# PEER block: 32 of 256 tokens taken out of the dense expert products, and V's rows as the stationary side

## The chip, the core and the metric

The kernel runs on one core of a Trainium2 chip. The core has five engines that run side by side: TensorE (PE; matrix products, with its weight loads shown apart as PEld), VectorE (DVE), ScalarE (ACT), GpSimd (POOL) and SyncE (SP), which here only issues transfers. All DMA queues share 16 DMA engines. The metric is device time in microseconds (us) of one execution; less is better.

## The reference

One decoder block for 256 tokens of width 1024: two token mixers with gates and a residual, then an expert layer (PEER) and a final norm. The change concerns the expert layer:

```python
qh = (x_blk @ w_q).reshape(tc, PEER_HEADS, 2, PEER_HALF)
scores = jnp.einsum('thpc,hpnc->thpn', qh, skf)          # 8 heads x 2 x 128 keys
s_top, i_top = lax.top_k(scores, PEER_TOPK)              # 16 of 128, twice per head
cand = s_top[:, :, 0, :, None] + s_top[:, :, 1, None, :]
c_s, c_pos = lax.top_k(cand.reshape(...), PEER_TOPK)     # 16 of 256 pairs
e_idx = ...                                              # 16 of 16384 experts per head
g = jax.nn.softmax(c_s, axis=-1)
u, v = expert_u[e_idx], expert_v[e_idx]
a = jax.nn.gelu(jnp.einsum('td,thkd->thk', x_blk, u), approximate=False)
return jnp.einsum('thk,thkd->td', g * a, v)
```

So each token uses 128 of 16384 experts, each a row of U and a row of V of 1024 numbers. Everything is float32; the answer must hold to float32 products.

## The kernel before

The kernel doesn't fetch the chosen rows. It computes all 16384 experts for all 256 tokens, in 128 blocks of 128 experts, and multiplies by a weight that is zero where an expert was not chosen.

**Precision.** TensorE's fast format, f32r, keeps part of a float32. `split` (lines 92 to 100) makes a first part `hi` on ScalarE (line 96) and the rest `lo` = source - hi on VectorE or GpSimd (line 99). A product is the sum hi*hi + hi*lo + lo*hi.

**U pass** (lines 607 to 648). Per block b: `load` fetches 512 KB of U (SyncE's queue, four `raw` buffers) and splits it; `mm3` (line 112) does 24 products, 8 chunks of the width by 3, with U as the stationary side (128 columns of weights each) and the tokens `xh`, `xl` as the moving side (256 columns); ScalarE applies GELU into `W[:, b]` (128 experts by 256 tokens, kept in SBUF for all blocks). Between blocks VectorE works on the top-16 search (`topk_steps`): first tokens 128 to 255, then 0 to 127. An allowance per block, `EARLY_RATE` before the scatter and `TOPK_RATE` after it, sets how many steps of the search are written behind each block. VectorE's order is the written order here (`manual_schedule`); the other engines' queues are ordered by the scheduler. Until the scatter is written, the rest of every second block goes to GpSimd (line 613).

**Weights of experts.** For tokens 128 to 255 GpSimd scatters the 128 x 128 weights into a table `gd` in memory that is zero elsewhere (line 469: 128 indirect transfers, each head behind the one before). For tokens 0 to 127 `g_build` makes them on TensorE, four tokens a group: 32 groups, line 581, four products each, spread over the later blocks; `g_use` multiplies them into `W`.

**V pass** (lines 695 to 712). Per block: `weigh` fetches the table's part (line 663) and multiplies it into `W` for tokens 128 to 255 (line 667); `W[:, b]` is split into `xhi`, `xlo`; V's block is loaded and split into `whi`, `wlo`; 12 products (line 675) with `W` as the stationary side (128 tokens) and V as the moving side (512 columns) add up in four accumulators, tokens by width. The last three blocks' products are sorted by accumulator, and `finish` (residual, sum of squares, norm, output) of the first 128 tokens runs under the products of the second.

## Time and profile before

| | us |
|---|---|
| median of 3 runs (1012.6 to 1015.11) | 1013.67 |
| the profiled execution | 1012.72 |
| its span, first to last instruction | 1010.9 |
| TensorE busy in it | 986.2 |
| VectorE, ScalarE, GpSimd busy | 732.4, 580.8, 305.1 |

A timeline row has start, duration, engine, line, operation, tiles (out<-in), shape and how many were merged; in brackets, the idle time before it and who ended it. A source row has count, ns min/median/max and first and last start. A row by stretches has its bounds and length, then busy us (and instructions) of each engine in the order PE, PEld, DVE, ACT, POOL, or of those engines alone that have the line that was asked for (line 99: DVE, POOL), then TensorE's granted clock (1.00 is 2.4 GHz), the DMA engines' busy share and GB/s. A plain f32 product is recorded as two passes, an f32r product as one.

### The profile page before, as it was taken

How to read it: one execution, taken by the hardware profiler on the slowest of the kernel's cores; microseconds unless marked ns; L12 is line 12 of the kernel's file. 1: busy time of each engine (PE TensorE's matmuls, PEld its weight loads, DVE VectorE, ACT ScalarE, POOL GpSimd, SP SyncE). 2: the span in 40 equal slices, each digit the busy share in tenths (PEclk: the TensorE clock that was granted, in tenths of full speed). 3: DMA queues.
4: the chain of work that ended last, by engine and by line, in shares of the span. 5: the costliest groups of instructions: out<-in, count | busy, mean ns of one | idle time of the engine just before them, and what ended most of it. 6: DMA issues, size and time to landing. Idle time of an engine off the chain costs nothing.

```text
span 1010.9 us, 17560 instructions
## 1 busy us (share of the span) xinstructions
PE 986.2 (98%) x6571; PEld 891.0 (88%) x6571; DVE 732.4 (72%) x1417; ACT 580.8 (57%) x1042; POOL 305.1 (30%) x210
## 2 busy tenths in 40 slices
PE   8999999999998999999999999999999999999996
PEld 7898899799998999999999999888888888888884
DVE  6566767764888988779789898766666666666665
ACT  5564546543564555778778777544444444444444
POOL 0000000000344878877877876001011010101010
PEclk9999999999999999999999999999999999999998
DMA  7667685545554877767667666766666666666662
GB/s 242 216 210 246 193 262 180 179 146 168 160 180 148 208 188 188 169 167 169 166 150 186 155 180 162 235 213 215 208 214 210 214 208 215 208 221 210 213 211 73
DMA packets 73557, 194.23 MB, mean 192 GB/s; under 512 B 25472, under 2 KB 25984, under 8 KB 73344
## 3 DMA queue, kind: packets, MB, share of 16 engines
q1 hardware_dynamic: 50400, 181.95, 57.3%
q0 software_dynamic: 21504, 8.47, 7.1%
q10 hardware_dynamic: 1568, 2.70, 0.8%
q8 instruction: 51, 0.84, 0.3%
q14 instruction: 34, 0.28, 0.1%
HBM read 183.58 MB, written 9.50 MB: 191 GB/s over the span
## 4 chain that ended last, share of the span: by engine, by line
PE 89%; DVE 5%; issue 2%; ACT 2%; DMA 1%; POOL 1%; ACTq 0%; DVEq 0%; POOLq 0%
PE pj L112 44%; PE acc L675 35%; PE pj L231 5%; DVE wlo L99 1%; PE gp L581 1%; ACT whi L96 1%; PE sps L412 1%; ACT JR L573 1%; POOL wlo L99 1%; DVE W L456 0%; DMA W<-in_consts_dram 0%; PE s L302 0%; DMA ident<-in_consts_dram 0%; PE tp L165 0%; PE z L250 0%
## 5 line engine op out<-in xcount | busy, mean ns | idle before, releaser
L96 ACT CAST whi<-raw 128x1024 fp32r<-128x1024 f32 x327 | 343.5, 1051 | 353.2 <-issue 195.9
L99 DVE TENSOR_TENSOR wlo<-raw,whi 128x1024 fp32r<-128x1024 f32 x315 | 386.4, 1228 | 168.4 <-ACT whi L96 164.0
L112 PE MATMUL pj<-xh,whi 128*128 128x256 f32 x1280 | 310.4, 282 | 2.9 <-ACT whi L96 2.9
L112 PE MATMUL pj<-xl,whi 128*128 128x256 f32 x1280 | 308.7, 280 | 0.1
L469 POOL DMA_INDIRECT gd<-gS,iS x128 | 239.0, 1867 | 66.9 <-issue 36.3
L112 PEld LDWEIGHTS pj<-xh,whi 128*128 128x128 f32 x1280 | 241.3, 189 | 5.0 <-ACT whi L96 4.1
L112 PEld LDWEIGHTS pj<-xl,whi 128*128 128x128 f32 x1280 | 241.5, 189 | 0.7 <-DVE xl L172 0.4
L112 PE MATMUL pj<-xh,wlo 128*128 128x256 f32 x1280 | 180.5, 282 | 6.0 <-DVE wlo L99 3.8
L112 PEld LDWEIGHTS pj<-xh,wlo 128*128 128x128 f32 x1280 | 162.1, 188 | 10.1 <-DVE wlo L99 6.8
L675 PE MATMUL acc<-whi,xlo 128*128 128x512 f32 x512 | 161.7, 395 | 0.7 <-DVE xlo L99 0.7
L675 PE MATMUL acc<-wlo,xhi 128*128 128x512 f32 x512 | 161.4, 394 | 0.0
L675 PE MATMUL acc<-whi,xhi 128*128 128x512 f32 x512 | 139.9, 395 | 0.5 <-ACT xhi L96 0.5
L663 POOL DMA_DIRECT2D gq<-gd x64 | 34.5, 540 | 326.3 <-DVE W L667 306.2
L675 PEld LDWEIGHTS acc<-whi,xlo 128*128 128x128 f32 x512 | 96.3, 188 | 24.1 <-DVE xlo L99 1.6
L99 POOL TENSOR_TENSOR wlo<-raw,whi 128x1024 fp32r<-128x1024 f32 x12 | 30.9, 2574 | 285.5 <-ACT whi L96 271.7
L675 PEld LDWEIGHTS acc<-whi,xhi 128*128 128x128 f32 x512 | 96.3, 188 | 23.5 <-ACT xhi L96 1.1
L675 PEld LDWEIGHTS acc<-wlo,xhi 128*128 128x128 f32 x512 | 96.5, 188 | 22.5
L620 ACT ACTIVATE W<-pj 128x256 f32<-128x256 f32 (+24 forms) x128 | 44.3, 347 | 19.2 <-PE pj L112 19.1
L99 DVE TENSOR_TENSOR xlo<-W,xhi 128x256 fp32r<-128x256 f32 x128 | 53.6, 419 | 0.7 <-ACT xhi L96 0.7
L96 ACT CAST xhi<-W 128x256 fp32r<-128x256 f32 x128 | 51.5, 403 | 2.3 <-DVE W L667 2.3
L573 ACT ACTIVATE JR<-iota,njT 128x128 fp32r<-128x128 f32 x128 | 41.1, 396 | 0.0
L577 DVE TENSOR_TENSOR B<-I,g 128x1024 fp32r<-128x1024 f32 x32 | 39.3, 1227 | 1.1
(185 smaller groups left out, 917.4 us busy)
## 6 DMA issues: line engine op xcount, KB each, us to landing
raw<-in_ut_dram SPq DMA_DIRECT2D x128, 512.0 KB
raw<-in_v_dram SPq DMA_DIRECT2D x128, 512.0 KB
raw<-in_wf_dram SPq DMA_DIRECT2D x72, 512.0 KB
gd<-zfill SPq DMA_DIRECT2D x16, 512.0 KB
gq<-gd POOLq DMA_DIRECT2D x64, 128.0 KB
gd<-gS,iS POOLq DMA_INDIRECT x128
h<-in_x_dram SPq DMA_DIRECT2D x4, 256.0 KB
sks<-in_skt_dram ACTq DMA_DIRECT2D x1, 1024.0 KB
```

The costliest lines, as they stand in the source:

```text
L96: last_hi = nc.scalar.copy(hi, src)
L99: last_lo = rest.tensor_sub(lo, src, hi.bitcast(F32))
L112: nc.tensor.matmul(o, a, b, start=first and i == 0, stop=last and i == len(seq) - 1)
L231: nc.tensor.matmul(pss[tt], a[:, c, s], w[:, cc], start=k == 0 and c == 0, stop=k == 2 and c == 7)
L412: nc.tensor.matmul(sps[tt][:, mm], qt[:, tt * P:(tt + 1) * P], sks[:, m], start=True, stop=True)
L469: d = nc.gpsimd.indirect_dma_start(gd[:, :], bass.IndirectOffsetOnAxis(ap=iS[:, k:k + 1], axis=0), gS[:, k:k + 1], None, compute_op=ALU.add)
L573: nc.scalar.activation(JR[:, q], iota, AF.Abs, bias=njT[:, 4 * g + q:4 * g + q + 1])
L577: nc.vector.tensor_tensor(B, I.unsqueeze(2).to_broadcast([P, 4, 2, P]), g2[:, :, ts_].bitcast(F32).rearrange("p l t -> p t l").unsqueeze(3 ...
L581: nc.tensor.matmul(gp[:, q].rearrange("p l i -> p (l i)"), JR[:, q], B[:, q].rearrange("p l i -> p (l i)"), start=True, stop=True)
L620: gl = nc.scalar.activation(W[:, b, nd:T], ps[:, nd:T], AF.Gelu)
L663: ld = nc.gpsimd.dma_start(gq[0], gd3[:, b * P:(b + 2) * P].rearrange("j (i t) -> j i t", i=2))
L675: nc.tensor.matmul(acc[tt][hf], lhs[:, s], rhs[:, hs], start=order == 0 and b == 0, stop=order == 2 and b == NB - 1)
```

## The change

Tokens 0 to 31 leave both dense passes.

- **U pass**: the moving side is tokens 32 to 255, 224 columns; `W` has 224 columns per block, and the search's scratch in it moves. 24 groups of weights are built instead of 32. GpSimd has the rest of every block until the scatter is written, and `EARLY_RATE` is 2.4 instead of 1.45.
- **Behind the search of tokens 0 to 127**: expert numbers, gates and the normed rows of the 32 tokens are written to memory and read back spread over 128 partitions (16 tokens x 8 heads, two such groups).
- **V pass**: V's block is the stationary side, the tokens the moving side. First and rest of `W[:, b]` lie side by side in `xw`, so that `whi` meets both in one product of 448 columns, and `wlo` meets the first in one of 224; 16 products per block, into eight accumulators, width by tokens. `whi` and `wlo` have a third buffer in every third block. `xw` of block b+1 is prepared while block b runs, and the table's parts are weighed two blocks at a time.
- **The 32 tokens**: 64 gathers of 128 rows of U or V (512 KB each) on GpSimd's queue, two row buffers, one step per 1.81 blocks. VectorE multiplies and sums a row with the token (line 749), or adds a weighted row (line 761); 16 products with `sel` (128 x 16) sum the heads into the accumulators.
- **End**: each accumulator is copied (`gather_up`), turned back to tokens by width with two transposes and added to `h` (`finish`); the norm follows for all tokens at once.

```diff
@@ constants
-EARLY_RATE = 1.45
-PT = 128
+EARLY_RATE = 2.4
+S = 32
+ND = T - S
+PT = P - S
+X0 = ND - P
+GS = P // 8
@@ behind the search of tokens 0 to 127
+                    for dst, src in ((e_dr, eu), (w_dr, ge)):
+                        nc.sync.dma_start(dst.rearrange("(t e) k -> t (e k)", e=NH), src[0:S])
@@ U pass
-                    mm3(ps[:, :T], [(u_h[:, c], u_l[:, c], xh[:, c], xl[:, c]) for c in range(8)])
+                    mm3(ps[:, :ND], [(u_h[:, c], u_l[:, c], xh[:, c, S:], xl[:, c, S:]) for c in range(8)])
                     if b + 1 < NB:
-                        nxt = load(ut[b + 1], [P, 8, P], rest=nc.vector if scattered or b % 2 else nc.gpsimd)
+                        nxt = load(ut[b + 1], [P, 8, P], rest=nc.vector if scattered else nc.gpsimd)
...
+                            for e in range(NH):
+                                nc.sync.dma_start(x_dr.rearrange("(t e) (a b) -> e t a b", e=NH, a=8)[e], sxr)
+                            for dst, src in ((places, e_dr), (gates, w_dr)):
+                                nc.sync.dma_start(dst, src.rearrange("(g p) k -> p g k", g=ng))
...
-            with tc.issue_after(gl.ins):
-                nc.scalar.preload_act_table_set("natural_log_exp_and_others")
@@ V pass
+        def prepare(b):
+            w = (vp if b == NB - 1 else xsp).tile([P, 2, ND], F32R, name="xw", tag="xw")
+            nc.scalar.copy(w[:, 0], W[:, b])
+            with tc.issue_after(last_lo.ins):
+                nc.vector.tensor_sub(w[:, 1], W[:, b], w[:, 0].bitcast(F32))
+            return w
...
-            lhs, rhs = ((w_h, v_h), (w_l, v_h), (w_h, v_l))[order]
-            nc.tensor.matmul(acc[tt][hf], lhs[:, s], rhs[:, hs], start=order == 0 and b == 0,
-                             stop=order == 2 and b == NB - 1)
+            if order == 0:
+                nc.tensor.matmul(acc[c][:, S:S + 2 * ND], v_h[:, cs], w.rearrange("p a b -> p (a b)"),
+                                 start=b == 0, stop=False, skip_group_check=True)
+            else:
+                nc.tensor.matmul(acc[c][:, S:S + ND], v_l[:, cs], w[:, 0], start=False, stop=b == NB - 1,
+                                 skip_group_check=True)
...
+                    rows[n] = vp.tile([P, D], F32, name="rows", tag="rows", bufs=2)
+                    nc.gpsimd.indirect_dma_start(rows[n][:, :], None, (u_rows if kind == "u" else v_rows)[:, :],
+                                                 bass.IndirectOffsetOnAxis(ap=places[:, g, k:k + 1], axis=0))
...
+                        nc.vector.scalar_tensor_tensor(r, r, 1.0, xr, op0=ALU.mult, op1=ALU.mult,
+                                                       accum_out=a[:, g, k:k + 1])
...
+                        nc.scalar.activation(a[:, g], a[:, g], AF.Gelu)
+                        nc.vector.tensor_mul(a[:, g], a[:, g], gates[:, g])
+                        if g == ng - 1:
+                            nc.scalar.preload_act_table_set("natural_log_exp_and_others")
...
+                        nc.vector.scalar_tensor_tensor(sm, r, a[:, g, k:k + 1], sm, op0=ALU.mult, op1=ALU.add)
...
+                        nc.tensor.matmul(acc[c][:, g * GS:(g + 1) * GS], sm[:, c * P:(c + 1) * P], sel,
+                                         start=False, stop=True, skip_group_check=True)
@@ end
+            rest = vp.tile([P, T], F32, name="rest", tag="rest", bufs=3)
+            nc.gpsimd.memset(rest[:, :S], 0.0)
+            nc.scalar.copy(rest[:, S:], acc[c][:, T:T + ND])
+            nc.vector.tensor_add(rest, rest, acc[c][:, :T])
...
+                nc.tensor.transpose(tp[:, tt * P:(tt + 1) * P], rest[:, tt * P:(tt + 1) * P], ident)
+            nc.vector.tensor_add(h[:, :, cs], h[:, :, cs], tp[:, :T].rearrange("p (a b) -> p a b", a=2))
+            for tt in range(2):
+                nc.scalar.activation(sqs, h[:, tt, cs], AF.Square, accum_out=sq[:, tt, c:c + 1])
...
+        nc.scalar.activation(r, ss, AF.Ln)
+        nc.scalar.activation(r, r, AF.Exp, scale=-0.5)
```

The order of instructions moves in three places.

**Start of the U pass.** VectorE before, around the places of the scatter (`iS`); `wlo` is a rest of U's block, the steps on `W` are the search:

```order
L99 TENSOR_TENSOR wlo<-raw,whi 128x1024
L542 TENSOR_TENSOR W<-W 128x8x128
L542 TENSOR_TENSOR W<-W 128x8x64
L542 TENSOR_TENSOR W<-W 128x8x32
L543 TENSOR_TENSOR W<-W 128x128
L547 COPY gS<-W 128x128
L548 SCALAR_TENSOR_TENSOR W<-W 128x128
L549 TENSOR_SCALAR iS<-W,pcol 128x128
L99 TENSOR_TENSOR wlo<-raw,whi 128x1024
```

and VectorE now, at the same steps:

```order
L560 TENSOR_TENSOR W<-W 128x8x128
L560 TENSOR_TENSOR W<-W 128x8x64
L560 TENSOR_TENSOR W<-W 128x8x32
L561 TENSOR_TENSOR W<-W 128x128
L565 COPY gS<-W 128x128
L566 SCALAR_TENSOR_TENSOR W<-W 128x128
L567 TENSOR_SCALAR iS<-W,pcol 128x128
L472 MAX W<-sc_87 128x8 x2
L474 MAX_INDEX W<-W,sc_87 128x8 x2
L477 MATCH_REPLACE sc_87<-W,sc_87 128x128 x2
L109 TENSOR_TENSOR wlo<-raw,whi 128x1024
```

No rest of U stands among the search of the second 128 tokens any more; the first, that of block 15, stands behind half a head of the next search. GpSimd's queue before, from the rests on:

```order
L99 TENSOR_TENSOR wlo<-raw,whi 128x1024 x11
L469 DMA gd<-gS,iS 2097152x1
L99 TENSOR_TENSOR wlo<-raw,whi 128x1024
L469 DMA gd<-gS,iS 2097152x1 x127
L663 DMA gq<-gd 128x256 x64
```

and now (`rows` and `xr` are the gathers' and the token's buffers):

```order
L109 TENSOR_TENSOR wlo<-raw,whi 128x1024 x14
L487 DMA gd<-gS,iS 2097152x1 x128
L695 DMA gq<-gd 128x256 x5
L738 DMA rows<-in_ur_dram,places 128x1024 x2
L747 DMA xr<-xd 128x1024
L773 MEMSET rest 128x32 x3
L695 DMA gq<-gd 128x256 x2
L738 DMA rows<-in_ur_dram,places 128x1024 x2
```

All 14 rests stand ahead of the scatter, and the gathers share the queue with the table's parts from then on.

**A block of the V pass.** TensorE before, one block (accumulators are tokens by half the width):

```order
L675 MATMUL acc_8209<-whi,xhi 128x512
L675 MATMUL acc_8210<-whi,xhi 128x512
L675 MATMUL acc_8211<-whi,xhi 128x512
L675 MATMUL acc_8212<-whi,xhi 128x512
L675 MATMUL acc_8209<-whi,xlo 128x512
L675 MATMUL acc_8210<-whi,xlo 128x512
L675 MATMUL acc_8209<-wlo,xhi 128x512
L675 MATMUL acc_8210<-wlo,xhi 128x512
L675 MATMUL acc_8211<-whi,xlo 128x512
L675 MATMUL acc_8212<-whi,xlo 128x512
L675 MATMUL acc_8211<-wlo,xhi 128x512
L675 MATMUL acc_8212<-wlo,xhi 128x512
```

and now, the end of one block and the start of the next (accumulators are an eighth of the width by tokens):

```order
L720 MATMUL acc_8107<-xw,whi 128x448
L720 MATMUL acc_8108<-xw,whi 128x448
L723 MATMUL acc_8101<-xw,wlo 128x224
L723 MATMUL acc_8102<-xw,wlo 128x224
L723 MATMUL acc_8103<-xw,wlo 128x224
L723 MATMUL acc_8104<-xw,wlo 128x224
L723 MATMUL acc_8105<-xw,wlo 128x224
L723 MATMUL acc_8106<-xw,wlo 128x224
L723 MATMUL acc_8107<-xw,wlo 128x224
L723 MATMUL acc_8108<-xw,wlo 128x224
L720 MATMUL acc_8101<-xw,whi 128x448
L720 MATMUL acc_8102<-xw,whi 128x448
```

Products of 448 and of 224 columns come in runs of eight, each with V's columns as weights of its own. VectorE before, a block and the start of the next:

```order
L99 TENSOR_TENSOR wlo<-raw,whi 128x1024
L99 TENSOR_TENSOR xlo<-W,xhi 128x256
L667 TENSOR_TENSOR W<-W,gq 128x128
L99 TENSOR_TENSOR wlo<-raw,whi 128x1024
L99 TENSOR_TENSOR xlo<-W,xhi 128x256
```

and now, with the gathered rows' multiplies:

```order
L702 TENSOR_TENSOR W<-W,gq 128x2x128
L749 SCALAR_TENSOR_TENSOR rows,a<-rows,xr 128x1024
L709 TENSOR_TENSOR xw<-W,xw 128x224
L109 TENSOR_TENSOR wlo<-raw,whi 128x1024
L709 TENSOR_TENSOR xw<-W,xw 128x224
L109 TENSOR_TENSOR wlo<-raw,whi 128x1024
L702 TENSOR_TENSOR W<-W,gq 128x2x128
L749 SCALAR_TENSOR_TENSOR rows,a<-rows,xr 128x1024
```

The multiply of a gathered row stands ahead of the next block's `xw` and of V's next rest.

**The end.** TensorE before, from the last block's products on:

```order
L675 MATMUL acc_8210<-wlo,xhi 128x512
L675 MATMUL acc_8211<-whi,xlo 128x512
L675 MATMUL acc_8211<-wlo,xhi 128x512
L675 MATMUL acc_8212<-whi,xlo 128x512
L675 MATMUL acc_8212<-wlo,xhi 128x512
L773 UNCONDITIONAL_BRANCH
```

and now (`tpv` is the transposes' bank):

```order
L720 MATMUL acc_8107<-xw,whi 128x448
L723 MATMUL acc_8107<-xw,wlo 128x224
L720 MATMUL acc_8108<-xw,whi 128x448
L783 MATMUL tpv<-ident,rest 128x128 x2
L723 MATMUL acc_8108<-xw,wlo 128x224
L720 MATMUL acc_8108<-xw,whi 128x448
L783 MATMUL tpv<-ident,rest 128x128 x2
L723 MATMUL acc_8108<-xw,wlo 128x224
L783 MATMUL tpv<-ident,rest 128x128 x12
L908 UNCONDITIONAL_BRANCH
```

Two pieces are turned between the last accumulator's products, six behind them. ScalarE before, from the squares on:

```order
L96 CAST whi<-raw 128x1024
L96 CAST xhi<-W 128x256 x2
L684 ACTIVATE o,st<-h 128x512 x4
L134 ACTIVATE st<-st 128x1
L135 ACTIVATE st<-st 128x1
L134 ACTIVATE st<-st 128x1
L135 ACTIVATE st<-st 128x1
L689 ACTIVATE o<-h,st 128x512
L691 DMA out_dram<-o 128x512
L689 ACTIVATE o<-h,st 128x512
```

and now:

```order
L774 COPY rest<-acc_8107 128x224
L786 ACTIVATE sqs,sq<-h 128x128 x2
L774 COPY rest<-acc_8108 128x224
L786 ACTIVATE sqs,sq<-h 128x128 x12
L830 ACT_TABLE_LOAD
L830 ACTIVATE st<-st 128x2
L831 ACT_TABLE_LOAD
L831 ACTIVATE st<-st 128x2
L841 ACTIVATE o<-h,st 128x512 x2
L842 DMA out_dram<-o 128x512 x2
```

Twelve squares stand behind the last copy, and a table load ahead of each of the two steps of the norm. Line 651's table load at the end of the U pass is gone; that of line 755, which is written in the V pass, stands at the start of ScalarE's queue:

```order
L42 ACT_TABLE_LOAD
L70 DMA gts<-in_gt_dram 128x16
L71 DMA ident<-in_consts_dram 128x128
L755 ACT_TABLE_LOAD
L181 CAST xh<-xt 128x4x128 x2
```

It stands ahead of the first copy there, and none stands between the last GELU and the end.

## Rows read from the trace of the kernel before

**Rows 1.** The page's busy shares, and its chain of waits by engine and line.

```profile
PE 986.2 (98%) x6571; PEld 891.0 (88%) x6571; DVE 732.4 (72%) x1417; ACT 580.8 (57%) x1042; POOL 305.1 (30%) x210
...
PE pj L112 44%; PE acc L675 35%; PE pj L231 5%; DVE wlo L99 1%; PE gp L581 1%; ACT whi L96 1%; PE sps L412 1%; ACT JR L573 1%; POOL wlo L99 1%; DVE W L456 0%; DMA W<-in_consts_dram 0%; PE s L302 0%; DMA ident<-in_consts_dram 0%; PE tp L165 0%; PE z L250 0%
```

**Rows 2.** Timeline of TensorE: first of U, first of V, last product.

```profile
251.12 0.36 PE L112 MATMUL pj<-xh,whi 128*128 128x256 f32 x1
...
642.63 0.74 PE L675 MATMUL acc<-whi,xhi 128*128 128x512 f32 x2 [0.34 <-ACT xhi L96]
...
1001.14 0.39 PE L675 MATMUL acc<-wlo,xhi 128*128 128x512 f32 x1
```

**Rows 3.** Timeline of TensorE, two U blocks; then the chain's groups (start, us).

```profile
278.13 1.10 PE L112 MATMUL pj<-xh,wlo 128*128 128x256 f32 x8
...
280.93 1.10 PE L112 MATMUL pj<-xh,wlo 128*128 128x256 f32 x8
...
600.74 0.48 PE gp L581 x4
```

**Rows 4.** Timeline of TensorE, the first four products of two V blocks.

```profile
799.64 1.10 PE L675 MATMUL acc<-whi,xhi 128*128 128x512 f32 x4
...
802.43 1.09 PE L675 MATMUL acc<-whi,xhi 128*128 128x512 f32 x4
```

**Rows 5.** Timeline of weight loads behind a stall, cut after one, after two.

```profile
327.34 0.19 PEld L112 LDWEIGHTS pj<-xh,wlo 128*128 128x128 f32 x1 [1.96 <-POOL wlo L99]
...
327.34 0.30 PEld L112 LDWEIGHTS pj<-xh,wlo 128*128 128x128 f32 x2 [1.96 <-POOL wlo L99]
```

**Rows 6.** Timeline of TensorE: four passes of plain f32, 128 columns.

```profile
250.75 0.60 PE L412 MATMUL sps<-sks,qt 128*128 128x128 f32 x4
```

**Rows 7.** Busy in the search's stretch, all and line 99; timelines of GpSimd, VectorE.

```profile
254.20:322.40 68.20, 64.96 (x547) 63.99 (x546) 63.26 (x236) 39.61 (x56) 25.54 (x10) 1.00 0.55 172
...
254.20:322.40 68.20, 15.47 (x12) 25.54 (x10) 1.00 0.55 172
...
300.17 2.42 POOL L99 TENSOR_TENSOR wlo<-raw,whi 128x1024 fp32r<-128x1024 f32 x1 [2.98 <-PE pj L112]
...
300.25 2.42 DVE L518 TENSOR_SCALAR W<-W 128x128 uint32<-128x128 uint32 x1
302.60 0.22 DVE L519 TENSOR_SCALAR W<-W 128x128 uint32<-128x128 uint32 x1
...
322.40 2.50 POOL L469 DMA_INDIRECT gd<-gS,iS  x1 [7.12 <-DVE iS L549]
```

**Rows 8.** The scatter's line: ns min/median/max, starts; its waits (us, times).

```profile
L469 POOL DMA_INDIRECT gd<-gS,iS x128: 1537/1743/2561, 322.4 to 621.4; - x128
...
  DMA gd<-gS,iS: 23.4, 8
```

**Rows 9.** Timeline of VectorE, one V block.

```profile
803.29 1.23 DVE L99 TENSOR_TENSOR wlo<-raw,whi 128x1024 fp32r<-128x1024 f32 x1 [1.03 <-ACT whi L96]
804.44 0.42 DVE L99 TENSOR_TENSOR xlo<-W,xhi 128x256 fp32r<-128x256 f32 x1
804.77 0.29 DVE L667 TENSOR_TENSOR W<-W,gq 128x128 f32<-128x128 f32 x1
```

**Rows 10.** Two stretches; the last columns are TensorE's clock, DMA share, GB/s.

```profile
97.00:99.00 2.00, 2.00 (x16) 1.38 (x15) 0.77 (x1) 0.14 (x1) 0.00 (x0) 1.00 1.05 410
700.00:800.00 100.00, 100.00 (x432) 81.09 (x431) 63.46 (x108) 48.48 (x73) 9.38 (x18) 1.00 0.67 212
```

**Rows 11.** Timeline of ScalarE in the tail; then its table load, by line.

```profile
1002.17 0.63 ACT L684 ACTIVATE o<-h 128x512 f32<-128x512 f32 x1
...
1002.80 0.61 ACT L684 ACTIVATE o<-h 128x512 f32<-128x512 f32 x1
...
1006.35 0.72 ACT L689 ACTIVATE o<-h,st 128x512 f32<-128x512 f32 x1 [0.46 <-DVE st L139]
...
L651 ACT ACT_TABLE_LOAD x1 | 1.3, 1283 | 0.0
```

More of the change, by code (lines that the diff above doesn't have):

```diff
@@ new lines, in block_kernel, with products @@
+        acc = [psm.tile([P, 512], F32, name=f"acc{c}", tag="pj") for c in range(4)]
+        acc += [psv.tile([P, 512], F32, name=f"acc{c}") for c in range(4, 8)]
+        def products(b, c, parts, order):
+            v_h, v_l, w = parts
+            cs = slice(c * P, (c + 1) * P)
+            if order == 0:
[4 more added lines that the diff above has]
+                                 skip_group_check=True)
@@ L696, in block_kernel @@
+        kept = []
+        steps = fetched_steps()
+        done = 0
+        fetch_weights(0)
+        fetch_weights(2)
+        weigh(0)
+        w_next = prepare(0)
         for b in range(NB):
-            last = b >= NB - LAST + 2
-            weigh(b)
-            parts = (*load(v[b], [P, D], vp if last else splp), *split(W[:, b], [P, T], vp if last else xsp, "x"))
+            w = w_next
+            parts = (*load(v[b], [P, D], vp if b % 3 == (NB - 1) % 3 else splp), w)
             if b < NB - LAST:
-                for tt in range(2):
-                    for order in range(3):
-                        for hf in range(2):
-                            products(b, tt, hf, parts, order)
+                for order in range(2):
+                    for c in (range(8) if b else (4, 5, 6, 7, 0, 1, 2, 3)):
+                        products(b, c, parts, order)
@@ L705, in block_kernel @@
             else:
                 kept.append((b, parts))
[L707 to L712 removed]
+            if b + 1 < NB:
+                w_next = prepare(b + 1)
+            if b % 2 == 0:
+                weigh(b + 2)
+                fetch_weights(b + 4)
+            if b == 3:
+                nc.scalar.dma_start(gf, gf_row.partition_broadcast(P))
+                nc.scalar.dma_start(sel, consts[:, 1153:1153 + GS])
@@ new lines, in block_kernel @@
+            if b >= 1:
+                while done * (NB - 12) <= (b - 1) * 64:
+                    next(steps, None)
+                    done += 1
+        rests = []
+        for c in range(8):
+            for b, parts in kept:
+                for order in range(2):
+                    products(b, c, parts, order)
+            rests.append(gather_up(c))
+            if c > 1:
+                finish(c - 2, rests[c - 2])
+        finish(6, rests[6])
+        finish(7, rests[7])
+        ss, r, t = st[:, 20:22], st[:, 22:24], st[:, 24:26]
```

156 lines of the change are left out of this document (102 added, 54 removed).

## The prediction

> **What bounds the kernel now.** I read the page's busy shares and its chain of waits first. TensorE is busy for 986 of 1010.9 us, and 44% and 35% of the chain that ended last are the products of lines 112 and 675 [rows 1]. So time is won only where TensorE's own stream gets shorter, and lost where another engine overtakes it. Three timeline rows cut the span [rows 2]: the U pass begins at 251.12 and ends where the V pass begins, at 642.63 (391.5 us); V's last product ends at 1001.14 + 0.39 = 1001.53 (358.9 us); a tail of 9.4 us follows. What lies ahead of 251 is not touched.
>
> The pace within each pass: in the U pass eight products of 256 columns take 1.10 us and the last of them 0.28, so they start every (1.10 - 0.28) / 7 = 0.117 us; a block of 24 repeats after 2.80 [rows 3]. One group of four expert-weight products (line 581) puts 0.48 us between blocks [rows 3]. In the V pass a block of 12 products of 512 columns repeats after 2.79 us [rows 4], 0.2325 us each. Both are 0.455 ns per column. The U pass is thus 128 x 2.80 = 358.4, plus 32 groups x 0.48 = 15, plus 18 us of stalls.
>
> What a product costs besides its columns shows after a stall: the first weight load lasts 0.19 us, and two together 0.30, so the second starts 0.11 us behind the first, although nothing else was running [rows 5]. A load of 128 columns therefore keeps its path for 0.11 us. With 256 columns (0.117) that is just covered.
>
> **The change part by part.**
>
> *U pass, products.* The moving side falls from 256 to 224 columns; the weights stay 128 columns, 24 loads per block. By columns alone a product would take 224 x 0.455 = 0.102 us; its load takes 0.11. No row has an f32r product with fewer than 256 columns. The nearest with short columns are the plain f32 ones of 128: four start (0.60 - 0.27) / 3 = 0.11 us apart [rows 6], each behind its own load. I take 0.111: 3072 x (0.1167 - 0.111) = **-17.5 us**. The ends: 0.102 (-45) and 0.117 (0). Far above lies f32's own rate, two such passes per 128 columns, 1.7 ns per column, 0.38 us for 224. The Trainium skill, "TensorE: Matmul & The Clock Gate", section "Back-to-back issue gap", gives N / 2.4 + 2.5 ns per product. By that a product of 224 columns would take 96 ns; for 256 it gives 109, where this trace has 117, so the trace does not bear it out.
>
> *U pass, groups.* 24 instead of 32: 8 x 0.48 = **-3.8**.
>
> *U pass, start.* The order shows two moves. GpSimd has the first rests of 14 blocks in a row, instead of 12 spread over 23 blocks, and VectorE works through the top-16 search of the second 128 tokens with no rest of U between. VectorE was busy for 63.3 us from the search's start to the scatter's, 15.5 of them rests [rows 7]: 47.8 us remain. In them are waits for GpSimd: the bit shift of line 518 took 2.42 us and ended when GpSimd's rest, begun at 300.17, ended; its neighbour of the same size took 0.22 [rows 7]. GpSimd now has a rest in every block of 2.66 us, so I add some 6 us: the places are ready at 254.2 + 47.8 + 6 = 308, instead of 322. But block 15's rest is queued on VectorE behind all that and behind half a head's search: 308 + 1.2 + 1.2. TensorE then ends block 15 near 312, where an unhindered 16 blocks would end at 251.1 + 16 x 2.66 = 294. That is 18 us of stall; with some 9 left of the later ones, 27.5 against 18: **+10** (ends: 0 if the search runs without waits and overlaps, +18).
>
> *Scatter.* Its 128 issues ran from 322.4 to 621.4, and a head waits 23.4 / 8 = 2.9 us for the one before [rows 8]. Begun at 308 it has landed by about 308 + 299 + 5 = 612. The U pass ends at 251.1 + 128 x 2.664 + 24 x 0.48 + 27.5 = 631. Hidden by 19 us; that cover ends if products take 0.102.
>
> *V pass, products.* V's rows are weights now: per block eight products of 448 columns (both parts of the experts' activations side by side) and eight of 224. 8 x 448 x 0.4545 = 1.629 us, the loads under them; 8 x 0.111 = 0.888. Sum 2.517 against 2.79: 128 x 0.273 = **-35 us** (by columns alone 2.444; at 0.117, 2.565).
>
> *V pass, fetched tokens.* 16 f32 products with 16 columns, two passes of 0.11 us each [rows 6]: **+3.5**. On VectorE a block had 1.15 us for V's rest, 0.33 for the activations' rest and 0.29 for the weighing [rows 9]. Now 1.15 + 0.30 + 0.17 + 64 / 116 of one multiply over 1024 (1.2): 2.28 of 2.52 us, so it fits with a tenth to spare. The multiply waits for a gather, and V's rest and the next activations' rest stand behind it on VectorE, and TensorE behind those. With two row buffers a gather has two steps of 1.81 blocks, 9 us, to land; issue 1.74, landing 2.9 [rows 8] and 1.3 for 0.52 MB at 410 GB/s [rows 10] make 5.9.
>
> *V pass, transfers.* Per block 0.524 MB of V, 0.289 of gathered rows, 0.066 of weights: 0.879 MB in 2.517 us is 349 GB/s. The V pass before moved 212 GB/s with a busy share of 0.67, which is 316 at full share; but a two-microsecond stretch with the share full moved 410 [rows 10]. So it needs 2.14 to 2.78 us per block. I take the nearer to 410, since a queue that always holds work is the state of that stretch, and charge **+6** for single waits and +2 for the pass's start.
>
> *Tail.* ScalarE now copies eight accumulator pieces, and makes 16 squares of 128 columns. The order puts twelve of these squares behind the last copy, and six pairs of transposes behind the last product. The chain: the three `rest` buffers make the pieces 3 to 7 wait for the transposes of 0 to 4, last copy about 2.5 us after the last product; squares of 512 follow each other after 0.63 [rows 11], so at 128 about 0.31 each, so 12 x 0.31 = 3.7; then, where before the two small steps stood bare, each has a table load of 1.28 us in front [rows 11], because the order moved line 755's load to the program's start. 2.5 + 3.7 + 1.3 + 0.2 + 1.3 + 0.2 + 0.9 (four small VectorE steps) = 10.1, two output halves 1.45, and 3.8 from the last of these to the end as before (1007.1 to 1010.9, rows 11): 15.4 against 9.4, **+6**.
>
> Sum: U -17.5 - 3.8 + 10 = -11; V -35 + 3.5 + 8 = -23.5; tail +6; together -28.5. The span becomes 982; with the 1.8 us that lie around it (1012.7 - 1010.9) **984 us**. The profiled run lies 1 us below the median of the runs shown, 1013.67. Own range of this case, from the start's 0 to 18 and the single waits: 974 to 994.
>
> **Rivals.**
>
> *Columns alone set the pace* (0.102). For: both passes show the same 0.455 ns per column. Against: the 0.11 us between loads. U would end at 312 + 112 x 2.45 + 20 = 606, but the scatter and the first fetch of its weights hold V to 617: -25.5; V 128 x -0.346 + 11.5 = -33; tail +6: **960**. By the 96 ns of the Trainium skill ("TensorE: Matmul & The Clock Gate", section "Back-to-back issue gap") it would be about 940.
>
> *A shorter product buys nothing* (0.117, load plus a fixed handover), so that the change does not shorten the U pass. For: loads start just behind the product before. Against: f32 products with loads of the same width start every 0.11. U +4, V -29 + 11.5, tail +6: **1005**.
>
> *Transfers bind V.* For: 316 GB/s. Against: 410. At 2.70 us per block for the 117 blocks with gathers: V about -10, U -11, tail +6: **998**, up to 1008 at 2.78. The Trainium skill, "DMA: Bandwidth & Descriptors", section "Bandwidth", has 341 GB/s for 1 MB from memory. By that a block would take 2.58 us, 7 us more than forecast; the trace's stretches lie on both sides of it.
>
> *Slower than before: the gathers pace V.* Place: VectorE's multiply on a row buffer, with TensorE two rests behind. Two gathers per round trip L, so the 64 steps take 32 L. With U -11 and tail +6, V must lose 8 us to end above before: 32 L + 11 x 2.52 + 5.5 = 367, L = 10.4 us. My floor is 5.9; behind a load of V on shared engines it is 5.9 + 2.5, and with the multiply 9.6. So it decides just above what the rows show; at L = 12 V takes 417, and the whole **1066**.
>
> *f32r falls to f32's rate below 256 columns*: 3072 x (0.38 - 0.117) = +808 us in U alone. No row excludes it; none points to it.
>
> **How the numbers follow.** Forecast 0.50; columns alone 0.12; nothing gained per product 0.12; transfers 0.14; gathers 0.09; f32's rate 0.03. 0.3% (3 us) is what a measurement of this kernel tells from no change. Faster by more: the first two, most of the third and of the fourth (0.10 and 0.10): 0.82. Within: 0.05. Slower: 0.13. The range leaves out the last two cases and the lower edge of the second: 957 to 1010.
>
> **What would show it.** Products of line 112 that start every 0.111 us (0.102 and 0.117 are the rivals); a V block of 2.52 (2.44, 2.57, 2.70); the first scatter near 308 with a stall of TensorE ahead of block 15 that ends on a VectorE rest; no idle time of VectorE ahead of lines 749 and 761 that ends on a gather; two table loads after the last product and 15 us of tail. I am wrong if f32r has a threshold, if the search takes longer than 60 us, or if V's loads arrive late for ScalarE.

## The result: slightly slower, 1020.1 against 1014.2 us

The changed kernel takes 1020.11 us (median of 13 runs, 1015.64 to 1023.81), the kernel before 1014.17 (13 runs, 1011.14 to 1017.89). The ratio is 1.0056, with a 95% interval of 1.0039 to 1.0073. The forecast was 984, with 957 to 1010 as its range: wrong in size and in sign.

Busy shares and the end of the chain of waits, from the page of the changed kernel (its profiled run: span 1019.9 us):

```profile
PE 952.3 (93%) x7099; PEld 903.6 (89%) x7099; DVE 767.4 (75%) x1433; ACT 564.0 (55%) x1032; POOL 430.4 (42%) x288
...
PE acc L720 7%; PE acc L723 3%; DVE sm L761 1%; ACT sqs L786 0%; DVE xw L709 0%; PE acc L765 0%; ACT L831 0%; ACT L830 0%; ACT rest L774 0%; DVE o L843 0%; DVEq L908 0%; DVE h L784 0%; PE tpv L783 0%; ACT st L831 0%; ACT st L830 0%
```

Against [rows 1], TensorE has fallen from 98 to 93%, and a VectorE line, the multiply of a fetched row (L761), stands in the chain between products. The page's chain covers only the last eighth of the span, so I cut the span into the forecast's stages. First and last product of U, first of V, last of V, from TensorE's timeline:

```profile
253.12 0.35 PE L122 MATMUL pj<-xh,whi 128*128 128x224 f32 x1
...
622.66 0.94 PE L122 MATMUL pj<-xh,wlo 128*128 128x224 f32 x7
626.62 0.64 PE L720 MATMUL acc<-xw,whi 128*128 128x448 f32 x2 [3.02 <-DVE xw L709]
...
1002.39 0.35 PE L723 MATMUL acc<-xw,wlo 128*128 128x224 f32 x1
```

| stage, us | before | forecast | after |
|---|---|---|---|
| ahead of U | 251.1 | 251.1 | 253.1 |
| U pass | 391.5 | 380 | 370.5 |
| V pass with its start | 358.9 | 335 | 379.1 |
| tail | 9.4 | 15.4 | 17.2 |
| span | 1010.9 | 982 | 1019.9 |

In the last column the U pass ends with its last product, at 623.6; the 3.0 us that TensorE then waits are counted to V. U did better than forecast, the tail a little worse; V is 44 us off, more than the whole error of 38. (In other runs below U began between 251.6 and 254.9, so the 2 us ahead of it are a difference between single runs.)

**The products came out as forecast.** Three of U's products in a row, then two starts of V blocks behind the last fetched row, with the products between:

```profile
616.86 0.27 PE L122 MATMUL pj<-xl,whi 128*128 128x224 f32 x1
616.97 0.27 PE L122 MATMUL pj<-xh,whi 128*128 128x224 f32 x1
617.08 0.28 PE L122 MATMUL pj<-xl,whi 128*128 128x224 f32 x1
...
979.53 1.79 PE L720 MATMUL acc<-xw,whi 128*128 128x448 f32 x8
981.16 1.05 PE L723 MATMUL acc<-xw,wlo 128*128 128x224 f32 x8
982.04 0.78 PE L720 MATMUL acc<-xw,whi 128*128 128x448 f32 x3
```

Products of 224 columns start every 0.11 us; the V blocks repeat every 2.51 us (979.53, 982.04). But while rows are fetched, V's blocks are late: over the starts of the 128 blocks, 54.2 us are lost against 2.51 each, and 54 of the blocks are late by 0.2 to 2.1 us. The 3.4 us that the fetched tokens' own products take are among them.

**Who holds them.** From the list of waits, 720 to 972 us, which leaves out V's start (us in total, times, longest):

```profile
PEld acc L720 <- DVE xw L709: 32.0, 39, 1.4
...
ACT whi L106 <- DMA raw<-in_v_dram: 3.0, 2, 1.7
...
DVE sm L761 <- DMA rows<-in_v_dram,places: 0.3, 1, 0.3
```

The products wait for `xw`, the rest of W's block. ScalarE's wait for V's blocks (3.0 us) and VectorE's for fetched rows (0.3 us) are small beside it. (Ahead of 720 us it is mixed: from 624 to 720 TensorE's weight loads wait 13.1 us for `xw`, and VectorE waits 8.1 us for rows of U.) One late pair of blocks in the timeline of all engines shows why:

```profile
896.03 1.89 PE L720 MATMUL acc<-xw,whi 128*128 128x448 f32 x8 [0.84 <-DVE xw L709]
...
897.96 1.05 ACT L106 CAST whi<-raw 128x1024 fp32r<-128x1024 f32 x1 [2.29 <-PE acc L720]
...
898.64 1.82 PE L720 MATMUL acc<-xw,whi 128*128 128x448 f32 x8
898.91 0.37 ACT L707 CAST xw<-W 128x224 fp32r<-128x224 f32 x1
899.04 1.23 DVE L109 TENSOR_TENSOR wlo<-raw,whi 128x1024 fp32r<-128x1024 f32 x1 [1.63 <-ACT whi L106]
...
900.18 0.42 DVE L702 TENSOR_TENSOR W<-W,gq 128x256 f32<-128x256 f32 x1
...
900.52 1.28 DVE L761 SCALAR_TENSOR_TENSOR sm<-rows,a,sm 128x1024 f32<-128x1024 f32 x1
...
901.71 0.39 DVE L709 TENSOR_TENSOR xw<-W,xw 128x224 fp32r<-128x224 f32 x1
...
902.15 1.88 PE L720 MATMUL acc<-xw,whi 128*128 128x448 f32 x8 [0.81 <-DVE xw L709]
```

Read it as a loop over two blocks. The block that starts at 896.03 frees a buffer of V's first part; ScalarE casts the block three further on into it (897.96), VectorE makes its rest (899.04), weighs (900.18), multiplies a fetched row (900.52), and only then makes the rest of `xw` (901.71) for which the block of 902.15 waits. That is 6.12 us where two blocks need 5.02. The input of that rest, ScalarE's cast, was done at 898.91 + 0.37 = 899.28. And it could not come earlier than the block of 896.03 ended, because `xw` has two buffers. VectorE meanwhile stood idle for 1.63 us in this pair, and for 1.2 to 1.7 us in most others.

### The profile page after: what moved, and what is told of

It is laid out like the page before. It is cut to its first block, busy times and chain, and to the rows that moved or that the text cites. A ratio compares the mean times of both kernels' runs of the same rounds, so it can differ in the third digit from the quotient of the medians.

```text
span 1019.9 us, 18735 instructions
## 1 busy us (share of the span) xinstructions
PE 952.3 (93%) x7099; PEld 903.6 (89%) x7099; DVE 767.4 (75%) x1433; ACT 564.0 (55%) x1032; POOL 430.4 (42%) x288
## 3 DMA queue, kind: packets, MB, share of 16 engines
q0 software_dynamic: 31008, 43.07, 15.9%
## 5 line engine op out<-in xcount | busy, mean ns | idle before, releaser
L122 PE MATMUL pj<-xh,whi 128*128 128x224 f32 (+1 forms) x1280 | 304.5, 279 | 5.8 <-ACT whi L106 5.8
L122 PE MATMUL pj<-xl,whi 128*128 128x224 f32 (+1 forms) x1280 | 303.8, 279 | 0.1
L720 PE MATMUL acc<-xw,whi 128*128 128x448 f32 x1024 | 237.7, 372 | 39.1 <-DVE xw L709 38.3
L487 POOL DMA_INDIRECT gd<-gS,iS x128 | 242.8, 1897 | 70.8 <-issue 35.8
L720 PEld LDWEIGHTS acc<-xw,whi 128*128 128x128 f32 x1024 | 182.9, 188 | 60.7 <-DVE xw L709 45.1
L122 PE MATMUL pj<-xh,wlo 128*128 128x224 f32 (+1 forms) x1280 | 175.8, 279 | 3.7 <-DVE wlo L109 3.7
L723 PEld LDWEIGHTS acc<-xw,wlo 128*128 128x128 f32 x1024 | 135.4, 191 | 3.5
L723 PE MATMUL acc<-xw,wlo 128*128 128x224 f32 x1024 | 137.5, 273 | 0.0
L738 POOL DMA_INDIRECT rows<-in_v_dram,places x32 | 57.8, 1805 | 52.7 <-DVE sm L761 36.9
L738 POOL DMA_INDIRECT rows<-in_ur_dram,places x32 | 53.7, 1678 | 49.7 <-DVE rows L749 47.6
L709 DVE TENSOR_TENSOR xw<-W,xw 128x224 fp32r<-128x224 f32 x128 | 49.3, 386 | 0.2
L761 DVE SCALAR_TENSOR_TENSOR sm<-rows,a,sm 128x1024 f32<-128x1024 f32 x30 | 38.4, 1280 | 0.4 <-DMA rows<-in_v_dram,places 0.3
```

The source lines that it names most:

```text
L122: nc.tensor.matmul(o, a, b, start=first and i == 0, stop=last and i == len(seq) - 1)
L487: d = nc.gpsimd.indirect_dma_start(gd[:, :], bass.IndirectOffsetOnAxis(ap=iS[:, k:k + 1], axis=0), gS[:, k:k + 1], None, compute_op=ALU.add)
L709: nc.vector.tensor_sub(w[:, 1], W[:, b], w[:, 0].bitcast(F32))
L720: nc.tensor.matmul(acc[c][:, S:S + 2 * ND], v_h[:, cs], w.rearrange("p a b -> p (a b)"), start=b == 0, stop=False, skip_group_check=True)
L723: nc.tensor.matmul(acc[c][:, S:S + ND], v_l[:, cs], w[:, 0], start=False, stop=b == NB - 1, skip_group_check=True)
L738: nc.gpsimd.indirect_dma_start(rows[n][:, :], None, (u_rows if kind == "u" else v_rows)[:, :], bass.IndirectOffsetOnAxis(ap=places[:, g, k ...
```

## The experiments

"Lost in V" is, for each run, the starts of the 128 blocks of V against 2.51 us each. Times are medians; the kernel before, run beside them, took 1013.2 to 1014.8 us.

| run | time, us | ratio to before (95%) | lost in V, us |
|---|---|---|---|
| the change | 1020.1 | 1.0056 (1.0039 to 1.0073) | 54.2 |
| e1_rest_first | 1004.7 | 0.9885 (0.983 to 0.9939) | 37.6 |
| e2_rows_only | 988.5 | 0.9756 (0.9727 to 0.9784) | 20.9 |
| e3_multiplies_only | 1017.8 | 1.0055 (1.0035 to 1.0075) | 54.9 |
| e4_no_fetch | 970.8 | 0.9582 (0.9561 to 0.9602) | 8.3 |
| e5_three_xw | 996.9 | 0.9822 (0.9784 to 0.986) | 32.6 |
| e6_four_rows | 979.7 | 0.9677 (0.9645 to 0.9709) | 17.0 |
| e7_alternate | 1029.6 | 1.0153 (1.0122 to 1.0184) | 60.9 |
| e8_all | 975.9 | 0.9629 (0.9599 to 0.9658) | 11.2 |
| e9_pace | 998.3 | 0.9829 (0.9811 to 0.9847) | 15.4 |
| e10_squares | 973.6 | 0.9605 (0.959 to 0.9619) | 12.7 |
| e11_both | 998.5 | 0.9836 (0.9822 to 0.9851) | 14.9 |
| e12_pace_16 | 976.3 | 0.9623 (0.9606 to 0.9639) | 15.9 |

### Order, rows and multiplies taken apart (e1 to e4)

```diff
 def prepare(b):                                  # e1_rest_first
-        nc.vector.tensor_sub(w[:, 1], W[:, b], w[:, 0].bitcast(F32))
+        last_rest = nc.vector.tensor_sub(w[:, 1], W[:, b], w[:, 0].bitcast(F32))
...
-    with tc.issue_after(last_lo.ins):            # at both multiplies
+    with tc.issue_after(last_rest.ins):
```

> One edit: the multiply of a fetched row (L749, L761) is placed behind the newest rest of W's block (xw, L709) on VectorE instead of in front of it. All work and all transfers stay. In the changed kernel the 128 blocks of V's products lose 54.5 us against 128 x 2.51 us, and most of the late ones start when xw is done. Theory Q (order on VectorE: the rest that TensorE waits for stands behind a 1.2 us multiply): the late blocks fall from about 1.0 us late to under 0.2, the sum of lost time from 54.5 to under 20 us, and the time to 980 to 990 us. Theory L (VectorE simply has too much to do in these stretches, in whatever order): the lost time moves to another instruction, 1008 to 1020 us. Theory D (the transfers, 16 engines 82 to 90% busy, hold up V's blocks): no change, 1015 to 1024 us.

```diff
-    nc.vector.scalar_tensor_tensor(sm, r, a[:, g, k:k + 1], sm, ...)               # e2_rows_only, at both multiplies
+    nc.vector.scalar_tensor_tensor(sm[:, :16], r[:, :16], a[:, g, k:k + 1], sm[:, :16], ...)
```

> The rows are fetched as before, but only 16 of each row's 1024 columns are multiplied, so the output of 32 tokens is left out: the transfers without VectorE's share (64 x 1.2 us). Theories Q and L: blocks of 2.51 to 2.6 us, lost time in V's products 5 to 15 us, 973 to 985 us. Theory D: the lost time stays above 40 us, 1010 to 1022 us.

```diff
-    rows[n] = vp.tile([P, D], F32, name="rows", tag="rows", bufs=2)                # e3_multiplies_only
-    nc.gpsimd.indirect_dma_start(rows[n][:, :], None, ...)
+    rows[n] = still[n % 2]
```

> The multiplies stay, on tiles that are filled with zeros once, and nothing is fetched (the output of 32 tokens is left out): VectorE's share without the transfers. Theories Q and L: the steady late blocks stay at 0.6 to 1.0 us, lost time 38 to 50 us, 1006 to 1018 us (what goes is the first 20 us of V's products, where transfers were waited for). Theory D: blocks of 2.51 us, lost time under 10 us, 970 to 978 us.

```diff
-    while done * (NB - 12) <= (b - 1) * 64:                                        # e4_no_fetch
-        next(steps, None)
-        done += 1
```

> No row is fetched and none multiplied; eight products of zeros for each group stand in their place (the output of 32 tokens is left out). All theories: blocks of 2.51 us throughout, lost time under 6 us, 965 to 972 us; this is the floor which the fetched rows are measured against. Were V's blocks late here too, the cause would lie in the new form of the products themselves and not in the fetched rows (time above 990 us).

One row of the stretch 720 to 920 us from each: the change, then e1, e2, e3 and e4 (busy us and count of TensorE, its loads, VectorE, ScalarE, GpSimd; granted clock; DMA share; GB/s).

```profile
720.00:920.00 200.00, 180.74 (x1106) 167.12 (x1105) 155.57 (x225) 91.40 (x139) 89.39 (x72) 1.00 0.88 304
```

```profile
720.00:920.00 200.00, 186.97 (x1152) 175.67 (x1152) 162.76 (x232) 96.23 (x145) 86.66 (x75) 0.98 0.92 321
```

```profile
720.00:920.00 200.00, 194.18 (x1230) 183.73 (x1229) 135.72 (x249) 101.51 (x153) 75.72 (x81) 1.00 0.94 337
```

```profile
720.00:920.00 200.00, 180.34 (x1103) 166.72 (x1103) 154.42 (x223) 90.66 (x137) 18.24 (x34) 1.00 0.67 201
```

```profile
720.00:920.00 200.00, 200.00 (x1263) 190.70 (x1262) 130.67 (x193) 101.93 (x155) 20.55 (x39) 0.98 0.75 228
```

Without fetched rows (e4) the new form of the products runs without a pause, so it is not at fault; 6.8 of the 8.3 us that it loses stand around its own products of zeros, which come in one row (they are why it lost more than the 6 I had allowed). With the multiplies alone (e3) TensorE loses as much as with everything: in the order of the change the transfers cost nothing further. With the rows alone (e2) it still loses 20.9 us, 12.6 more than e4 and more than the 15 I had allowed. So there are two causes, and the first covers the second. Of the 54.2 us e1 wins back 16.6, where I had expected 35 and more. Theory Q was right on the cause and wrong on what would come next:

```profile
DVE sm L764 <- DMA rows<-in_v_dram,places: 13.4, 10, 3.6
DVE rows L752 <- DMA rows<-in_ur_dram,places: 5.8, 6, 1.5
```

These waits of e1 (720 to 950 us) were 0.3 us in the change over that stretch. One of them in e1's timeline:

```profile
901.17 1.70 POOL L741 DMA_INDIRECT rows<-in_v_dram,places  x1 [0.90 <-DVE sm L764]
...
904.67 1.28 DVE L764 SCALAR_TENSOR_TENSOR sm<-rows,a,sm 128x1024 f32<-128x1024 f32 x1
...
906.22 1.70 POOL L741 DMA_INDIRECT rows<-in_v_dram,places  x1 [0.90 <-DVE sm L764]
...
910.99 1.28 DVE L764 SCALAR_TENSOR_TENSOR sm<-rows,a,sm 128x1024 f32<-128x1024 f32 x1 [3.60 <-DMA rows<-in_v_dram,places]
...
914.10 3.33 PE L723 MATMUL acc<-xw,whi 128*128 128x448 f32 x8 [3.88 <-DVE xw L712]
```

With two row buffers a fetch starts when the multiply before last has ended, and the row is due two multiplies later. The row fetched from 901.17 on was due at 907.4, when VectorE began to wait, 6.2 us after its issue began; it was there at 910.99, and `xw` and the product came 3.9 us late. (The eight products of 914.10 then took 3.33 us instead of 1.88; the last section says why.) The list of transfers gives the median from issue to landing, for rows of U 6.3 us in the change and 7.9 in e1:

```profile
rows<-in_ur_dram,places POOLq DMA_INDIRECT x32, 6.3
```

```profile
rows<-in_ur_dram,places POOLq DMA_INDIRECT x32, 7.9
```

V's own loads land later too, after 6.3 us (median) instead of 4.2, and the core moves 321 GB/s instead of 304. That the faster TensorE goes, the more loads and rows hold each other up, is the likely reading; no run separates it. The multiply then waits on VectorE with the next rests behind it.

### More buffers (e5, e6, e8)

```diff
-    xsp = ctx.enter_context(tc.tile_pool(name="xsplit", bufs=2))      # e5_three_xw (on the change)
+    xsp = ctx.enter_context(tc.tile_pool(name="xsplit", bufs=3))
```

> One edit to the changed kernel: three buffers for the two parts of W's block (xw) instead of two; the multiplies stand in front of the rest of xw as in the changed kernel. With two buffers xw of a block can't be begun before TensorE has finished the block two before, so it has one block (2.51 us) for a cast, a 1.2 us rest of V, a multiply and its own rest. Theory Q (it is this short chain, not the amount of work): with a buffer more it has two blocks, the late blocks of 0.6 to 1.0 us go as they did in the run with the multiply behind the rest, and the time is 998 to 1006 us, what then remains being waits for fetched rows. If the place of the multiply alone matters, whatever the buffers: no change, 1015 to 1024 us.

```diff
-    ... tag="rows", bufs=2)                                           # e6_four_rows (on e1)
+    ... tag="rows", bufs=4)
-    gather(0)
+    for n in range(3):
+        gather(n)
...
-        gather(n + 1)
+        gather(n + 3)
```

> The kernel with the multiply behind the rest (1004.7 us) with four buffers for fetched rows instead of two, and three fetches under way instead of one. There VectorE waited 19.2 us in 720 to 950 us for a row that was still being fetched, with TensorE's next xw behind it, and 25.7 us were lost behind block 24. Theory T (a fetch takes longer than the step allows now and then, and only one is under way): these waits fall under 4 us, the time to 984 to 992 us. Theory D (the 16 DMA engines are 91 to 93% busy there, so that V's own blocks come late once rows are fetched earlier): the waits move to ScalarE's cast of V's blocks, 998 to 1006 us.

```diff
-    nc.scalar.preload_act_table_set("natural_log_exp_and_others")     # e8_all (on e6, with e5)
+    with tc.issue_after(ga.ins):                                      # ga: the last Gelu
+        nc.scalar.preload_act_table_set("natural_log_exp_and_others")
```

> Together: the multiply behind the rest, three buffers for xw, four for fetched rows with three fetches under way, and ScalarE's table load of the logarithm put behind its last Gelu (in the changed kernel it had been moved to the start, and two loads of 1.28 us stand in the tail). Theory T with Q: V's blocks at 2.51 us with under 12 us lost over 128, the tail 17.5 - 2.6 = 14.9 us, 976 to 986 us. Theory D: the transfers bind, blocks of 2.6 to 2.7 us, 994 to 1004 us.

e5 leaves the multiply in front and still gains 21.6 us in V: the place hurts only because the chain from one free buffer of `xw` to the next product is short. Over the V pass the weight loads' wait for `xw` falls from 45.1 us to 8.5. And of the 32.6 us that e5 still loses, 18.8 stand at one place:

```profile
793.41 3.60 PE L765 MATMUL acc<-sel,sm 128*128 128x16 f32 x16 [12.88 <-DVE sm L761]
```

These are the products that sum the first group of fetched tokens. With the third buffer TensorE has run ahead of the rows and must wait here for the last of them; from 786 to 800 us the granted clock is 0.50 (1.2 GHz), and the next two blocks start 16.5 and 2.3 us late. So the waits for rows, 33.1 us on VectorE in this run, no longer come through `xw`, but are paid once where the sum is needed.

e6 gains a further 20.6 us over e1, and its stretch reads:

```profile
720.00:920.00 200.00, 198.99 (x1258) 188.76 (x1259) 177.85 (x253) 104.30 (x158) 91.95 (x81) 1.00 0.96 345
```

TensorE is full again, with VectorE at 89% and 345 GB/s. Theory T holds, with a time below its range, and D falls: the transfers are near their end (0.96 of the engines' time) but do not bind. e8 came out as T with Q had it; its tail, 16.1 us behind the start of the last product, is 1.4 us shorter than the 17.5 of the change, not 2.6.

### U's start and the tail (e7, e9 to e12)

```diff
-EARLY_RATE = 2.4                                                      # e7_alternate (on the change)
+EARLY_RATE = 1.45
-    nxt = load(ut[b + 1], [P, 8, P], rest=nc.vector if scattered else nc.gpsimd)
+    nxt = load(ut[b + 1], [P, 8, P], rest=nc.vector if scattered or b % 2 else nc.gpsimd)
```

> The changed kernel with GpSimd's part undone: first rests of U alternate between VectorE and GpSimd and the search is paced as before (EARLY_RATE 1.45). In the changed kernel U's first 34 blocks lose 15.6 us, before the change 7 to 8. If the price of that part is what the forecast said (about 10 us lost at U's start for an earlier scatter): U's start loses 7 to 8 us; the scatter begins near 320 instead of 308 us, and as it takes some 306 us it ends near 626 us, behind the end of U's products near 615 us, so V's products begin near 632 us and nothing is gained, 1018 to 1030 us. If the scatter doesn't hold V's start: 1010 to 1014 us.

```diff
-EARLY_RATE = 2.4                                                      # e9_pace (on e8)
+EARLY_RATE = 2.0
```

> The kernel with the four edits of V's products and the tail (975.9 us), with the search at U's start paced at 2.0 a block instead of 2.4. In it U's first 34 blocks lose 13 to 16 us, in three stops of about 4.1 us each at which ScalarE stands at a step of the search whose input VectorE hasn't reached (4.9, 2.7 us of waiting), with the casts of U's blocks behind it. Theory P (the code paces ScalarE's part of the search faster than VectorE does its own): the stops shrink, 4 to 8 us lost, U's products end 7 to 10 us earlier, near 613 us. Theory S (VectorE's search and so the scatter begin at the same time as now, 307 us, and the scatter's 306 us end near 613 us and hold V's start): V's products still begin near 619 to 622 us and the time falls by 2 to 5 us only, to 971 to 974 us. Without S: 966 to 969 us. If the pace isn't the cause, U's start loses what it lost: 976 us.

Both went another way than expected, by the same cause (e7's time lies in its range, for another reason). From the list of waits of e7 (330 to 356 us), and of e9 (300 to 342 us) with GpSimd's timeline:

```profile
PE pj L122 <- POOL wlo L109: 13.2, 1, 13.2
```

```profile
PE pj L122 <- POOL wlo L109: 28.7, 1, 28.7
```

```profile
308.87 1.78 POOL L487 DMA_INDIRECT gd<-gS,iS  x1 [6.63 <-DVE W L472]
310.94 1.60 POOL L487 DMA_INDIRECT gd<-gS,iS  x1 [0.30 <-issue]
...
332.36 2.92 POOL L109 TENSOR_TENSOR wlo<-raw,whi 128x1024 fp32r<-128x1024 f32 x1
```

A rest that GpSimd was to make stood behind 12 (e7) or 13 (e9) issues of the scatter, at 1.85 us each. In the kernel before one such rest stood behind a single issue. So neither run measures the pace. Without its one stop of 13.2 us e7 loses 13.3 us in U besides the products and groups, the change 15.9, so the change's two edits here cost U about 3 us; it is more if what the lower clock behind that stop cost (0.50 from 350 to 354 us) is taken off as well. And they belong together: at 2.4 a block all rests of GpSimd end before the scatter.

```diff
     for tt in range(2):                                               # e10_squares (on e8)
-        nc.scalar.activation(sqs, h[:, tt, cs], AF.Square, accum_out=sq[:, tt, c:c + 1])
+        if tt:
+            nc.vector.scalar_tensor_tensor(sqv, h[:, tt, cs], 1.0, h[:, tt, cs], op0=ALU.mult,
+                                           op1=ALU.mult, accum_out=sq[:, tt, c:c + 1])
+        else:
+            nc.scalar.activation(sqs, h[:, tt, cs], AF.Square, accum_out=sq[:, tt, c:c + 1])
```

> The kernel with the four edits (975.9 us), with the squares of one of the two token halves on VectorE instead of ScalarE. In its tail ScalarE does squares of 0.43 us each without a pause for 5 us behind the last column's result, while VectorE has 3 us of nothing to do. If this row of squares sets the tail, its length falls by 2 to 2.5 us (from 16.1 to about 14 us behind the last product's start), 973 to 974 us; if VectorE's chain of sums does, nothing changes or it gets longer, 976 to 978 us.

e11 has both edits, the pace of e9 and the squares of e10:

> Both: the search at 2.0 a block and half of the squares on VectorE. With S: 969 to 972 us; without S: 964 to 967 us; each of the two gains adds to the other, since one lies before U's end and the other behind the last product.

```diff
-    nxt = load(ut[b + 1], [P, 8, P], rest=nc.vector if scattered else nc.gpsimd)    # e12 (on e11)
+    nxt = load(ut[b + 1], [P, 8, P], rest=nc.vector if scattered or b >= 16 else nc.gpsimd)
```

> The best kernel so far (973.6 us, four edits and half of the squares on VectorE) with the search at 2.0 a block, and the first rests of U's blocks go back to VectorE from block 17 on, so that no rest stands behind the scatter on GpSimd (with 2.0 alone two stood behind 13 of its transfers, and TensorE stopped for 30.7 us once). Theory P with S (the search's steps on ScalarE come too early at 2.4; the scatter, about 306 us from about 308 us on, holds V's start): U's start loses 6 to 9 us instead of 13.1, V's products begin at 617 to 621 us, 970 to 974 us. P without S: V begins at 613 to 616 us, 966 to 970 us. If VectorE, which has the search and now a rest more, is what holds U's start: it loses 12 to 16 us as before, 973 to 978 us.

e10's tail is 16.0 us against 16.1 in e8: VectorE's squares now end last, so the second answer of its expectation is the right one; its 973.6 us is the lowest time here, 2.3 us below e8, which its tail does not account for. (In the profiled runs V's first product waits 3.1 us in e8 and not at all in e10.) e11 repeats e9's stop. e12 puts the rests in front of the scatter: U loses 10.0 us instead of e10's 13.4, and nothing is gained, since V's first product comes 2.7 us behind U's end, at 621.4. Its scatter (first and last start), and its wait for the first weights (600 to 640 us):

```profile
L487 POOL DMA_INDIRECT gd<-gS,iS x128: 1547/1795/2582, 312.2 to 611.6; - x128
```

```profile
DVE W L702 <- DMA gq<-gd: 4.7, 1, 4.7
```

The scatter's issues take 299 us, the last comes 7 us ahead of U's end, and the weights can be fetched only when it has landed. In e10 the scatter had begun at 305.2, not 312.2, and V's first product did not wait. So a shorter U was worth nothing here: the scatter came later and holds V's start, as theory S had it, though the time, 976.3, is above the 970 to 974 that S with P gave and in the range of the third answer, whose loss at U's start (12 to 16 us) did not come.

## Why the prediction was wrong

- **U's products: right.** Forecast 0.111 us by the load, measured 0.11; the block 2.68 instead of 2.664, so -15.4 instead of -17.5. The rivals of 0.102 and 0.117 fall. The 96 ns that follow from the Trainium skill, "TensorE: Matmul & The Clock Gate", section "Back-to-back issue gap", which gives its formula for an isolated product, are not what these products take.
- **U's groups: right**, -4.0.
- **U's start: size right, place wrong.** Forecast +10; over U's first 34 blocks 7.7 us were lost before and 15.6 now, +7.9. The scatter began at 308.5, as forecast (308). But TensorE's stops are three of 2.8 to 3.7 us instead of one of 18, so that the size agrees is luck. At two of them ScalarE stands at a step of the search whose input VectorE has not reached, with the casts of U behind it:

```profile
269.68 1.99 ACT L528 CAST W<-W 128x1024 bf16<-128x1024 uint32 x2 [4.90 <-DVE W L474]
...
289.79 0.31 ACT L534 ACTIVATE W<-W 128x128 f32<-128x128 f32 x1 [2.71 <-DVE W L533]
```

  The third is the rest queued on VectorE that I had named.
- **U's later stops: missed.** I left them as they were; of 9.7 us 0.3 are left. With this U is 21 us shorter, not 11.
- **V's products: right**, 2.51 us, -35.8. The fetched tokens' own products took 1.70 us a group, 3.4 in all: right.
- **V, the fetched rows on VectorE: the step that failed.** "2.28 of 2.52 us, so it fits with a tenth to spare" adds up VectorE's work and takes the sum for the limit. The sum was right: e6 and e10 run V at 2.51 us a block with it. But what TensorE waits for is a chain, from the end of one product through a cast, a rest, a weighing and a multiply to the rest of `xw`, within the time that two buffers give. I had written that "V's rest and the next activations' rest stand behind it on VectorE, and TensorE behind those" and priced only the multiply's wait for its row, not the multiply itself standing there. For single waits I had put 6 us; the late blocks cost 50.8 (54.2 less 3.4 of the fetched tokens' own products), and with the multiplies alone (e3) as much.
- **V's transfers: the choice was right.** I took the demand of 349 GB/s for possible by [rows 10]; e6 kept 345 over 200 us. The 341 of the Trainium skill ("DMA: Bandwidth & Descriptors", section "Bandwidth") is 1% below that. The rival that transfers bind falls.
- **The gathers as pace: a smaller truth than the rival.** A row lands after 6.3 us (5.9 was my floor), and 7.9 once V runs faster; with the rows alone (e2) V took 342.5 us, less than before. But at V's start VectorE does wait for rows (8.1 us), which I had named as a sign against me, and with the multiplies out of the way the rows held back 20.6 us of e1.
- **V's start: +2 forecast**, 3.0 us of TensorE's wait measured, as the scatter ended late.
- **The tail: mechanism right, +7.8 instead of +6.** Both table loads stand there:

```profile
1009.64 0.31 ACT L786 ACTIVATE sqs<-h 128x128 f32<-128x128 f32 x1
...
1010.06 1.28 ACT L830 ACT_TABLE_LOAD   x1
...
1011.58 1.28 ACT L831 ACT_TABLE_LOAD   x1
1012.87 0.20 ACT L831 ACTIVATE st<-st 128x2 f32<-128x2 f32 x1
```

  I scaled a square from 0.63 us for 512 columns to 0.31 for 128. They follow each other every 0.43 us (1009.21, 1009.64), since reading the sum out takes 0.19 us for 128 columns as for the 512 of the kernel before: 12 x 0.12 = 1.4 us of the 1.8.

Against the rows of before: V's +20.2 us (products -35.8, the fetched tokens' 3.4, the rest late blocks and the start) take back U's -21.0, and tail and front make the difference. What stays open: why U's later stops went (from 330 us to U's end VectorE was 87% busy before and is 82% now, with eight groups fewer to build, but no run tests it), and how much the search's pace alone is worth, as no run changed it without moving the scatter too.

## What to carry to other kernels

An engine with a tenth to spare can still stop another: follow the chain from one freed buffer to the next product, in the order in which the engine has its work, and put what nobody waits for behind what somebody does, or give that chain a buffer more. Where one wait goes, look for the next behind it: here the order hid the latency of the fetch. Of the 54.2 us lost in V the order alone gave back 16.6 and a third `xw` buffer alone 21.6, but the order with four row buffers 37.2. The version with the multiply behind the rest, three buffers for `xw`, four for rows and the table load in its place ran at 975.9 us, 0.963 of the kernel before, and with half of the squares on VectorE at 973.6 (0.9605), below both kernels.
